# Putting three attention groups together: inside the attention stage, or after it

## The chip, the cores and the metric

The kernel runs on one core of a Trainium2 chip. Its time is the device time of one execution in microseconds (us). The core has five engines that matter here: TensorE (PE, with its weight loads shown as PEld), VectorE (DVE), ScalarE (ACT), GpSimd (POOL) and SyncE (SP), whose queue issues all transfers between HBM and the on-chip memory in this kernel.

## The reference, cut to what matters

One layer of a trunk: a normalised input, one wide projection, a state-space branch and an attention branch, both gated, merged and projected out. Sequence 2048, model width 1024. The attention branch has three groups of four heads (head size 128). The groups differ in how far apart their keys lie:

```
DILATION_PATTERNS = ((128, 1), (512, 4), (2048, 16))

for gi, (window, dilation) in enumerate(DILATION_PATTERNS):
    o, s = dilated_group_attention(q[:, :, gi], k[:, :, gi], v[:, :, gi], window, dilation)
    outs.append(o); lses.append(s)
alpha = softmax(stack(lses), axis=0)
y = sum(alpha[..., None] * outs, axis=0)          # the three groups of a head slot
...
y_a = y * silu(z_a)
```

A head slot j (0 to 3) is head j of all three groups. Its three outputs are summed with weights that come from the three softmax denominators, position by position, and the sum is multiplied by silu of a gate projection z_a.

## The kernel before, in words

Matrix products run in f32r, with each operand split into a high and a low part and three products in place of one. The normalised input stays on chip (`hhi`, `hlo`); weights come from HBM in raw tiles `w_raw` of 128x512, are split by ScalarE (high part, L67) and VectorE (low part, L68) into `w_hi` and `w_lo`, and are then used for products of 128x512 (`proj`, L132 to L143). A pair of weight strips is four raw tiles. The tag `w_raw` has two buffers, and so have `w_hi` and `w_lo` (two pairs). Tag `ev` (two buffers) serves the tiles that come from or go to HBM in the attention stage: V of a chunk (`load_split`, L842) and the output `acc` of a chunk (L928, L979).

The stages in order of the program: input and projections for the state-space branch, state-space scan with gate strips between, its output gate (glu), the attention stage, the z stage, the output stage.

- Attention stage: `for j in range(4): for g in range(3): self.unit(...)`. A unit (j, g) loads its Q and K weights (`pair`, L827) and goes through four chunks of 512 positions: K projection, V load, Q projection, scores (L914, L970), softmax (L887), transposes (L920 to L923, L973), products with V (L940, L978), then a store of the chunk's sums without denominator to HBM (`numd`, L963 or L981). At its end maxima and denominators go to HBM (`statd`, L871 to L885).
- z stage: `weights_of_groups` (L983) reads the statistics of a slot, works out the three weights per position and stores them in HBM (`fd`). `combine` (L1004) reads, for each quarter of 512 positions and each group, the sums (`cn`) and the weights spread over 128 partitions (`cf`), multiplies and adds on GpSimd (L1028 to L1031) and leaves the slot's whole result in an on-chip tile `cy` of 128x2048. In between, gate strips are projected: `tanh` strips, and `silu` strips (L682 to L699), whose banks are multiplied by a quarter of `cy` (L697) before they are stored to `ya`.

The order of instructions on each engine is made by a planner when the program is built: it follows the order of the program where nothing else decides, takes what is ready in its own reckoning of the time, and gives each tile one of the buffers of its tag. On the chip each engine works through its own list in that fixed order, and each instruction waits for those on other engines that it depends on. SP issues transfers in its own fixed order as well, and one that has to wait holds up those behind it.

Of the kernel before, what the change touches and what calls it, by code (L numbers as in the profile page):

```python
# [20 lines left out]
SEQ = 2048  # L21
# [18 lines left out]
class Builder:  # L40
# [641 lines left out]
    def gate_bank(self, ev, psum, w, s, q, dst, silu=False, factor=None):  # L682

        nc = self.nc
        t = {}

        def product():
            t["ps"] = psum.tile([128, 512], F32, tag="proj", name="proj")
            return self.proj(t["ps"], w, s, self.pos(q))

        def evict():
            e = t["e"] = ev.tile([128, 512], F32, tag="ev", name="ze" if silu else "ge")
            nc.scalar.activation(e, t["ps"], AF.Tanh, scale=0.5)  # L693
            if silu:
                nc.vector.scalar_tensor_tensor(e, e, 1.0, t["ps"], op0=ALU.add, op1=ALU.mult)
            if factor is not None:
                nc.vector.tensor_tensor(e, e, factor[:, q * 512 : q * 512 + 512], op=ALU.mult)  # L697

        return product, evict, lambda: nc.sync.dma_start(dst[q], t["e"])  # L699

# [202 lines left out]
    def banded_chunk(self, g, c, carry, qh, ql, kh, kl, vh, vl, prev, st, pool, ev, psum, dst):  # L903
        nc = self.nc
        ph, pl = (pool.tile([128, 8, 128], F32R, name=n) for n in ("ph", "pl"))
        for pair in range(2):
            s = psum.tile([128, 2, 256], F32, tag="s", name="s")
            t = psum.tile([128, 4, 128], F32, tag="t", name="t")
            lone = pair == 0 and not carry
            for h in range(2):  # L910
                b = 2 * pair + h
                k0 = 1 if b == 0 and not carry else b
                for n, (x, y) in enumerate(((qh, kh), (qh, kl), (ql, kh))):
                    nc.tensor.matmul(s[:, h], x[:, b], y[:, k0 : k0 + 2], start=n == 0, stop=n == 2)  # L914
            for h in range(2):
                b = 2 * pair + h
                first = b == 0 and not carry
                p = self.softmax(s[:, h], self.mask[:, 128:384] if first else self.mask[:, 0:256], 4 * c + b, st, pool)
                if first:
                    nc.tensor.transpose(t[:, 1], p[:, 0:128], self.ident)  # L920
                else:
                    nc.tensor.transpose(t[:, 2 * h], p[:, 0:128], self.ident)
                    nc.tensor.transpose(t[:, 2 * h + 1], p[:, 128:256], self.ident)  # L923
            i0 = 1 if lone else 0
            sl = slice(4 * pair + i0, 4 * pair + 4)
            self.split(ph[:, sl], pl[:, sl], t[:, i0:])
# [8 lines left out]
        def blocks(x):  # L935
            return x.rearrange("p b (i r) -> p b i r", r=width)
# [9 lines left out]
        nb = psum.tile([128, 4, 128], F32, tag="n", name="nb")  # L946
        pv(nb[:, 0:2], (vh[:, 1], vl[:, 1]), 3)
        pv(nb[:, 2:4], (vh[:, 2], vl[:, 2]), 5)
        lo = pool.tile([128, 4, 128], F32, name="nlo")
        if carry:  # L950
            nc.scalar.activation(lo[:, 0:2], na[:, 0::3], AF.Copy)
        else:
            nc.scalar.activation(lo[:, 1], na[:, 3], AF.Copy)
        nc.scalar.activation(lo[:, 2:4], nb[:, 1::2], AF.Copy)
        if carry:
            nc.vector.tensor_tensor(dest[:, 0], blocks(na[:, 2:3])[:, 0], blocks(lo[:, 0:1])[:, 0], op=ALU.add)
        else:
            nc.vector.tensor_copy(dest[:, 0], blocks(na[:, 2:3])[:, 0])
        nc.vector.tensor_tensor(dest[:, 1:3], blocks(nb[:, 0::2]), blocks(lo[:, 1:3]), op=ALU.add)
        nd = psum.tile([128, 2, 128], F32, tag="n", name="nd")  # L960
        pv(nd, (vh[:, 3], vl[:, 3]), 6)
        nc.vector.tensor_tensor(dest[:, 3], blocks(nd[:, 1:2])[:, 0], blocks(lo[:, 3:4])[:, 0], op=ALU.add)
        nc.sync.dma_start(dst, acc)  # L963

    def causal_chunk(self, c, q, k, v, st, pool, ev, psum, dst):
# [14 lines left out]
        nc.scalar.activation(acc, n.rearrange("p b i -> p (b i)"), AF.Copy)  # L980
        nc.sync.dma_start(dst, acc)  # L981

    def weights_of_groups(self, j, pool, statd, fd):  # L983

        nc = self.nc
        m = pool.tile([16, 6, 128], F32, name="cm")
        nc.sync.dma_start(m, statd[j].rearrange("g s (r i) -> r (g s) i", r=16))
        mx = pool.tile([16, 128], F32, name="cx")
        nc.vector.tensor_tensor(mx, m[:, 0], m[:, 2], op=ALU.max)
        nc.vector.tensor_tensor(mx, mx, m[:, 4], op=ALU.max)  # L990
        e = pool.tile([16, 3, 128], F32, name="ce")
        for g in range(3):
            nc.vector.tensor_tensor(e[:, g], m[:, 2 * g], mx, op=ALU.subtract)
        nc.scalar.activation(e, e, AF.Exp, scale=HEAD_SCALE)
        t = pool.tile([16, 3, 128], F32, name="ct")
        nc.vector.tensor_tensor(t, e, m[:, 1::2], op=ALU.mult)
        nc.vector.tensor_tensor(mx, t[:, 0], t[:, 1], op=ALU.add)
        nc.vector.tensor_tensor(mx, mx, t[:, 2], op=ALU.add)
        nc.vector.reciprocal(mx, mx)
        for g in range(3):  # L1000
            nc.vector.tensor_tensor(e[:, g], e[:, g], mx, op=ALU.mult)
        nc.sync.dma_start(fd[j].rearrange("g (r i) -> r g i", r=16), e)

    def combine(self, j, pool, numd, fd):  # L1004

        nc = self.nc
        y = pool.tile([128, SEQ], F32, name="cy", bufs=2)
        for q in range(4):
            qs = slice(512 * q, 512 * q + 512)
            yo = y[:, qs]  # L1010
            for g in range(3):
                f = pool.tile([128, 512], F32, name="cf", bufs=2)
                nc.sync.dma_start(f, fd[j, g : g + 1, qs].to_broadcast([128, 512]))
                n = pool.tile([128, 512], F32, name="cn", bufs=3)
                if g == 0:
                    src = numd[j, 0].rearrange("c p (h x) -> h p c x", h=4)[q]
                    nc.sync.dma_start(n.rearrange("p (c x) -> p c x", c=4), src)
                    vn = n.rearrange("p (c r i) -> p r c i", c=4, r=4)
                    vf, vy = (t.rearrange("p (r c i) -> p r c i", r=4, c=4) for t in (f, yo))
                elif g == 1:  # L1020
                    src = numd[j, 1].rearrange("c p (h x) -> h p c x", h=4)[q]
                    nc.sync.dma_start(n.rearrange("p (c x) -> p c x", c=4), src)
                    vn, vf, vy = n, f, yo
                else:
                    nc.sync.dma_start(n, numd[j, 2, q])
                    vn, vf, vy = n, f, yo
                if g == 0:
                    nc.gpsimd.tensor_tensor(vy, vn, vf, op=ALU.mult)  # L1028
                else:
                    nc.gpsimd.tensor_tensor(vn, vn, vf, op=ALU.mult)  # L1030
                    nc.gpsimd.tensor_tensor(vy, vy, vn, op=ALU.add)  # L1031
        return y


    def weight_tiles(self, pool, name, kt, cols=(0, D_MODEL)):
# [97 lines left out]
    def run(self, stop=None):  # L1133
        tc, nc, a = self.tc, self.nc, self.a
        with (
# [11 lines left out]
            numd = dp.tile([4, 3, 4, 128, 512], F32, name="numd")  # L1147
            statd = dp.tile([4, 3, 2, SEQ], F32, name="statd")
            fd = dp.tile([4, 3, SEQ], F32, name="fd")
            self.vd = dp.tile([3, SEQ, 512], F32, name="vd")  # L1150
            self.ident = cst.tile([128, 128], F32, name="ident")
            make_identity(nc, self.ident)
# [8 lines left out]
            with tc.tile_pool(name="w", bufs=2, **T) as wp, tc.tile_pool(name="ev", bufs=2, **T) as ev:  # L1161
# [35 lines left out]
                if stop == "glu":  # L1197
                    return
                with tc.tile_pool(name="at", bufs=1, **T) as ap:
                    self.mask = ap.tile([128, 384], F32, name="mask")  # L1200
                    nc.sync.dma_start(self.mask, a["mask"])
                    for j in range(4):
                        for g in range(3):
                            self.unit(j, g, wp, ap, ev, psum, numd, statd)
                if stop == "att":
                    return

                def emit(banks):
                    for bank in banks:
                        for step in bank:  # L1210
                            step()
# [1 line left out]
                def tanh(c):  # L1213
                    emit(self.tanh_pair(ev, psum, self.pair(wp, IDX_GA + c, IDX_GA + c + 1), gta[c : c + 2]))

                with tc.tile_pool(name="cb", bufs=1, **T) as cp:
                    for j in range(4):
                        self.weights_of_groups(j, cp, statd, fd)
                    for p in range(2):
                        y = [self.combine(j, cp, numd, fd) for j in (2 * p, 2 * p + 1)]  # L1220
                        if p == 0:
                            tanh(0)
                        tanh(2 + 2 * p)
                        i = IDX_ZA + 2 * p
                        emit(self.silu_pair(ev, psum, self.pair(wp, i, i + 1), ya[2 * p : 2 * p + 2], y))
                if stop == "ya":
                    return
                with tc.tile_pool(name="bs", bufs=1, **T) as bp:
# [14 lines left out]
def prepare(x, pre_norm_g, w_in, lambda_re, lambda_im, log_dt, b_re, b_im, c_re, c_im, d_skip, w_glu, b_glu,  # L1243
# [15 lines left out]
    never = np.full((128, 128), NEG)  # L1259
    mask = np.concatenate([before, own, never], 1)  # L1260
    diag0 = np.zeros((16, 8, 16))
    diag0[np.arange(16), 0, np.arange(16)] = 1.0
    return {
# [31 lines left out]
```

## Time and profile before

| | |
|---|---|
| time, median of 3 runs | 2094.47 us (2093.51 to 2095.44) |
| profiled execution | 2099.32 us, span 2097.5 us |
| TensorE busy | 2054.6 us (98%) |
| VectorE, ScalarE, GpSimd busy | 901.2, 592.8, 399.2 us |
| mean granted clock of TensorE | 0.992 |

The attention stage lies at about 750 to 1450 us of the span, the z stage at about 1450 to 1720. A busy TensorE is counted from the start of a product to its modelled end; products overlap, so a full share need not be its peak. The granted clock is 1.00 at 2.4 GHz.

### The profile page before, as it was taken

How to read it: one execution, taken by the hardware profiler on the slowest of the kernel's cores; microseconds unless marked ns; L12 is line 12 of the kernel's file. 1: busy time of each engine (PE TensorE's matmuls, PEld its weight loads, DVE VectorE, ACT ScalarE, POOL GpSimd, SP SyncE). 2: the span in 40 equal slices, each digit the busy share in tenths (PEclk: the TensorE clock that was granted, in tenths of full speed). 3: DMA queues.
4: the chain of work that ended last, by engine and by line, in shares of the span. 5: the costliest groups of instructions: out<-in, count | busy, mean ns of one | idle time of the engine just before them, and what ended most of it. 6: DMA issues, size and time to landing. Idle time of an engine off the chain costs nothing.

```text
span 2097.5 us, 30805 instructions
## 1 busy us (share of the span) xinstructions
PE 2054.6 (98%) x11668; PEld 1789.9 (85%) x11668; DVE 901.2 (43%) x2261; ACT 592.8 (28%) x1327; POOL 399.2 (19%) x384
## 2 busy tenths in 40 slices
PE   8999999999999999999999999999899999999998
PEld 6788888899999988888888888887677888999997
DVE  6882355645442234324424423433311226544434
ACT  6421122222223334334433433432111124112111
POOL 0002355555521210000000000000636101111111
PEclk9999999999999999999999999999999999999999
DMA  7334333343345521111111121113747336433323
GB/s 246 106 122 143 97 119 113 117 117 113 114 119 174 151 71 55 59 56 56 61 56 52 41 65 52 59 54 111 217 145 225 111 122 220 141 121 116 117 81 101
DMA packets 208372, 231.50 MB, mean 110 GB/s; under 512 B 24864, under 2 KB 142944, under 8 KB 207968
## 3 DMA queue, kind: packets, MB, share of 16 engines
q1 hardware_dynamic: 208224, 229.54, 35.5%
q8 instruction: 91, 1.49, 0.3%
q14 instruction: 57, 0.47, 0.1%
HBM read 146.52 MB, written 74.56 MB: 105 GB/s over the span
## 4 chain that ended last, share of the span: by engine, by line
PE 86%; DMA 7%; DVE 2%; ACT 1%; POOL 1%; issue 1%; SPq 1%; DVEq 0%; ACTq 0%; POOLq 0%
PE proj L141 46%; PE pv L163 13%; PE br L1089 8%; PE po L1108 8%; DMA cf<-fd 2%; PE glu L786 2%; PE s L914 2%; PE nb L940 1%; DMA raw<-in_wout_dram 1%; PE na L940 1%; DMA cn<-numd 1%; PE nc L978 1%; POOL cn L1030 1%; PE py L598 1%; PE s L970 1%; PE pd L561 1%
## 5 line engine op out<-in xcount | busy, mean ns | idle before, releaser
L141 PE MATMUL proj<-hhi,w_hi 128*128 128x512 f32 x1664 | 666.6, 402 | 25.6 <-ACT ge L693 15.5
L141 PE MATMUL proj<-hlo,w_hi 128*128 128x512 f32 x1664 | 660.9, 398 | 3.2 <-DVE hlo L68 2.7
L141 PE MATMUL proj<-hhi,w_lo 128*128 128x512 f32 x1664 | 660.1, 397 | 0.0
L141 PEld LDWEIGHTS proj<-hhi,w_hi 128*128 128x128 f32 x1664 | 316.2, 190 | 95.8 <-ACT ge L693 17.8
L141 PEld LDWEIGHTS proj<-hlo,w_hi 128*128 128x128 f32 x1664 | 316.1, 190 | 71.6 <-DVE hlo L68 3.4
L141 PEld LDWEIGHTS proj<-hhi,w_lo 128*128 128x128 f32 x1664 | 315.8, 190 | 65.5
L163 PE MATMUL pv<-w_hi,hhi 128*128 128x256 f32 x768 | 218.8, 285 | 0.0
L163 PE MATMUL pv<-w_hi,hlo 128*128 128x256 f32 x768 | 214.5, 279 | 0.0
L163 PE MATMUL pv<-w_lo,hhi 128*128 128x256 f32 x768 | 214.5, 279 | 0.0
L68 DVE TENSOR_TENSOR w_lo<-w_raw,w_hi 128x512 fp32r<-128x512 f32 (+1 forms) x130 | 108.1, 855 | 209.2 <-ACT w_hi L67 208.6
L163 PEld LDWEIGHTS pv<-w_hi,hhi 128*128 128x128 f32 x768 | 144.4, 188 | 0.6
L163 PEld LDWEIGHTS pv<-w_lo,hhi 128*128 128x128 f32 x768 | 144.4, 188 | 0.6
L163 PEld LDWEIGHTS pv<-w_hi,hlo 128*128 128x128 f32 x768 | 144.3, 188 | 0.0
L898 ACT ACTIVATE p<-p,nm 128x256 f32<-128x256 f32 (+1 forms) x192 | 89.5, 467 | 152.0 <-DVE nm L897 135.9
L892 DVE CUSTOM_DVE_ANT_0 p<-s,mask 128x256 f32<-128x256 f32 (+1 forms) x192 | 68.2, 376 | 147.1 <-PE t L973 68.7
L1092 POOL TENSOR_TENSOR gt<-gt 128x256 f32<-128x256 f32 x64 | 48.3, 759 | 386.1 <-DVE gt L1091 221.3
L67 ACT ACTIVATE w_hi<-w_raw 128x512 fp32r<-128x512 f32 (+1 forms) x130 | 77.1, 620 | 124.6 <-DMA w_raw<-in_wst_dram 87.5
L848 POOL CAST kh<-kh 128x128 fp32r<-128x128 f32 x12 | 3.6, 296 | 538.2 <-PE s L970 426.3
L1108 PE MATMUL po<-wout0h,mh 128*128 128x512 f32 x256 | 98.9, 392 | 1.6 <-ACT wout0h L67 1.4
L1108 PE MATMUL po<-wout0l,mh 128*128 128x512 f32 x256 | 99.8, 390 | 0.0
L1108 PE MATMUL po<-wout0h,ml 128*128 128x512 f32 x256 | 99.5, 390 | 0.0
L693 ACT ACTIVATE ge<-proj 128x512 f32<-128x512 f32 x64 | 37.8, 593 | 192.1 <-PE proj L141 136.9
(248 smaller groups left out, 3341.8 us busy)
## 6 DMA issues: line engine op xcount, KB each, us to landing
w_raw<-in_wst_dram SPq DMA_DIRECT2D x126, 256.0 KB
vd<-ve SPq DMA_DIRECT2D x48, 256.0 KB
numd<-acc SPq DMA_DIRECT2D x48, 256.0 KB
cn<-numd SPq DMA_DIRECT2D x48, 256.0 KB
cf<-fd SPq DMA_DIRECT2D x48, 256.0 KB
xT<-in_xT_dram SPq DMA_DIRECT2D x32, 256.0 KB
gts<-ge SPq DMA_DIRECT2D x32, 256.0 KB
sx<-sx SPq DMA_DIRECT2D x64, 128.0 KB
```

Source lines behind the costliest of these rows:

```text
L67: nc.scalar.activation(hi, src, AF.Copy)
L68: nc.vector.tensor_tensor(lo, src, raw(hi), op=ALU.subtract)
L141: last = nc.tensor.matmul(ps, st[:, k, cs], m, start=n == 0, stop=n == 23)
L163: last = nc.tensor.matmul(ps[:, o], st[:, k, rs], m[:, k], start=n == 0, stop=n == 23)
L786: nc.tensor.matmul(ps, st[:, k, cs], m[:, k], start=n == 0, stop=n == 11)
L892: nc.vector.tensor_tensor_reduce(p[:, :n], scores, mask, scale=1.0, scalar=-3.0e38, op0=ALU.add, op1=ALU.max, accum_out=st[:, 0, blk : blk ...
L898: nc.scalar.activation(p[:, :n], p[:, :n], AF.Exp, scale=HEAD_SCALE, bias=nm, accum_out=st[:, 1, blk : blk + 1])
L914: nc.tensor.matmul(s[:, h], x[:, b], y[:, k0 : k0 + 2], start=n == 0, stop=n == 2)
L940: nc.tensor.matmul(out, x, y[:, i0 : i0 + 2], start=n == 0, stop=n == 2)
L1089: nc.tensor.matmul(ps, st[:, k, cs], m[:, i, k], start=n == 0, stop=n == 11)
L1092: nc.gpsimd.tensor_tensor(gt[:, 0], gt[:, 0], gt[:, 1], op=ALU.add)
L1108: nc.tensor.matmul(po[b, half], st[:, k, bs], m[:, k, hs], start=k == 0 and n == 0, stop=k == 7 and n == 2,)
```

## The change

Combining moves into the attention stage: right behind the three units of slot j, `combine(j)` works out the weights, and for each of eight pieces of 256 positions and each group loads weights and sums into one tile, multiplies and adds on GpSimd, and stores the sum to HBM (`yad`). The tile of a piece takes tag `w_raw`. The z strips load the quarter that they need from `yad` into one of three buffers. The weights are worked out on 128 partitions of 16 positions, not 16 of 128. The first block of a sequence has 128 keys only, so its scores and mask are cut to 128 columns, and the third mask block goes. `nlo` shrinks to two blocks, used twice in a chunk.

```diff
-                nc.vector.tensor_tensor(e, e, factor[:, q * 512 : q * 512 + 512], op=ALU.mult)
+                nc.vector.tensor_tensor(e, e, factor(q), op=ALU.mult)
...
-                k0 = 1 if b == 0 and not carry else b
+                lead = b == 0 and not carry
+                out, ks = (s[:, h, :128], slice(1, 2)) if lead else (s[:, h], slice(b, b + 2))
                 for n, (x, y) in enumerate(((qh, kh), (qh, kl), (ql, kh))):
-                    nc.tensor.matmul(s[:, h], x[:, b], y[:, k0 : k0 + 2], start=n == 0, stop=n == 2)
+                    nc.tensor.matmul(out, x[:, b], y[:, ks], start=n == 0, stop=n == 2)
...
-        nc.scalar.activation(lo[:, 2:4], nb[:, 1::2], AF.Copy)
...
-        nc.vector.tensor_tensor(dest[:, 1:3], blocks(nb[:, 0::2]), blocks(lo[:, 1:3]), op=ALU.add)
+        nc.vector.tensor_tensor(dest[:, 1], blocks(nb[:, 0:1])[:, 0], blocks(lo[:, 1:2])[:, 0], op=ALU.add)
+        lo = pool.tile([128, 2, 128], F32, name="nlo")
+        nc.scalar.activation(lo, nb[:, 1::2], AF.Copy)
+        nc.vector.tensor_tensor(dest[:, 2], blocks(nb[:, 2:3])[:, 0], blocks(lo[:, 0:1])[:, 0], op=ALU.add)
...
+    def combine(self, j, wp, pool, numd, statd, fd, yd):
...
+        m = pool.tile([128, 6, 16], F32, name="cm")
+        nc.sync.dma_start(m, statd[j].rearrange("g s (p x) -> p (g s) x", x=16))
...
+        nc.sync.dma_start(fd[j].rearrange("g (p x) -> p g x", x=16), e)
         for q in range(4):
+            for o in (0, 256):
+                y = pool.tile([128, 256], F32, name="cy")
+                for g in range(3):
+                    r = wp.tile([128, 2, 256], F32, tag="w_raw", name="cnf", bufs=2)
+                    f, n = r[:, 0], r[:, 1]
+                    at = 512 * q + o
+                    nc.sync.dma_start(f, fd[j, g : g + 1, at : at + 256].to_broadcast([128, 256]))
+                    if g == 0:
+                        src = numd[j, 0].rearrange("c p (h x) -> h p c x", h=8)[2 * q + o // 256]
+                        nc.sync.dma_start(n.rearrange("p (c x) -> p c x", c=4), src)
...
+                        nc.gpsimd.tensor_tensor(vy, vn, vf, op=ALU.mult)
+                    else:
...
+                        nc.gpsimd.tensor_tensor(n, n, f, op=ALU.mult)
+                        nc.gpsimd.tensor_tensor(y, y, n, op=ALU.add)
+                nc.sync.dma_start(yd[j, q][:, o : o + 256], y)
...
                     for j in range(4):
                         for g in range(3):
                             self.unit(j, g, wp, ap, ev, psum, numd, statd)
+                        self.combine(j, wp, ap, numd, statd, fd, yad)
...
-                with tc.tile_pool(name="cb", bufs=1, **T) as cp:
-                    for j in range(4):
-                        self.weights_of_groups(j, cp, statd, fd)
+                with tc.tile_pool(name="za", bufs=1, **T) as zp:
+
+                    def mixed(j, q):
+                        f = zp.tile([128, 512], F32, name="cy", bufs=3)
+                        nc.sync.dma_start(f, yad[j, q])
+                        return f
...
-                        y = [self.combine(j, cp, numd, fd) for j in (2 * p, 2 * p + 1)]
```

## Rows read from the trace of the kernel before

**Rows 1.** The page, busy us of each engine, share of the span, instructions.

```profile
PE 2054.6 (98%) x11668; PEld 1789.9 (85%) x11668; DVE 901.2 (43%) x2261; ACT 592.8 (28%) x1327; POOL 399.2 (19%) x384
```

**Rows 2.** Windows of 50 us: stretch, length, busy per engine, clock, DMA share, GB/s.

```profile
850.00:900.00 50.00, 50.00 (x264) 42.25 (x263) 17.47 (x65) 18.95 (x54) 0.00 (x0) 1.00 0.20 64
...
1450.00:1500.00 50.00, 43.28 (x182) 35.10 (x183) 27.91 (x50) 7.39 (x15) 25.07 (x20) 0.97 0.66 190
1500.00:1550.00 50.00, 47.02 (x196) 38.32 (x195) 3.25 (x4) 6.98 (x12) 29.50 (x23) 0.93 0.73 212
1550.00:1600.00 50.00, 46.84 (x200) 38.30 (x199) 15.05 (x20) 6.87 (x12) 22.45 (x17) 0.97 0.53 163
1600.00:1650.00 50.00, 46.67 (x200) 38.26 (x200) 5.84 (x9) 9.33 (x16) 26.94 (x22) 0.97 0.70 209
1650.00:1700.00 50.00, 50.00 (x223) 41.40 (x222) 14.13 (x21) 8.81 (x15) 0.00 (x0) 1.00 0.26 90
```

**Rows 3.** Windows of 5 us in the z stage, the same columns.

```profile
1500.00:1505.00 5.00, 2.51 (x12) 1.73 (x10) 0.02 (x1) 0.68 (x2) 4.04 (x4) 0.95 0.89 215
1505.00:1510.00 5.00, 4.51 (x11) 3.55 (x12) 1.93 (x2) 1.55 (x3) 2.96 (x3) 0.50 1.02 348
```

**Rows 4.** Chain of waits, 1500 to 1520 us: start, us, what.

```profile
1511.92 4.34 DMA cf<-fd
```

**Rows 5.** Timeline of SP's queue, 780 to 860 us: start, us, instruction, count.

```profile
782.46 0.32 SPq L963 DMA_DIRECT2D numd<-acc  x1
784.44 0.37 SPq L100 DMA_DIRECT2D ev<-vd  x1
...
801.35 0.94 SPq L100 DMA_DIRECT2D w_raw<-in_wst_dram  x2
...
806.17 1.19 SPq L100 DMA_DIRECT2D w_raw<-in_wst_dram  x2
...
859.48 0.93 SPq L100 DMA_DIRECT2D w_raw<-in_wst_dram  x2
```

**Rows 6.** Timelines of VectorE and ScalarE, 778 to 863 us; in brackets idle before, and releaser.

```profile
778.20 0.69 DVE L68 TENSOR_TENSOR vl<-ev,vh 128x512 fp32r<-128x512 f32 x1 [0.80 <-ACT vh L67]
...
790.65 0.38 DVE L956 TENSOR_TENSOR acc<-na,nlo 128x128 f32<-128x128 f32 x1
...
858.09 1.15 ACT L67 ACTIVATE w_hi<-w_raw 128x512 fp32r<-128x512 f32 x2 [1.01 <-PE proj L141]
...
862.16 0.63 ACT L67 ACTIVATE w_hi<-w_raw 128x512 fp32r<-128x512 f32 x1 [0.17 <-DMA w_raw<-in_wst_dram]
```

**Rows 7.** Timeline, 1434 to 1458 us: the end of the last attention unit.

```profile
1434.57 0.58 ACT L862 ACTIVATE q<-proj 128x512 f32<-128x512 f32 x1
...
1439.24 1.05 PE L970 MATMUL s<-k,q 128*128 128x128 f32 x8
...
1441.00 0.40 ACT L898 ACTIVATE p<-p,nm 128x128 f32<-128x128 f32 x1 [1.99 <-DVE nm L897]
...
1448.43 0.34 SPq L885 DMA_DIRECT2D statd<-stt  x1
1448.87 0.37 SPq L987 DMA_DIRECT2D cm<-statd  x1
...
1456.21 0.32 SPq L1002 DMA_DIRECT2D fd<-ce  x1
...
1457.78 0.85 SPq L1013 DMA_DIRECT2D cf<-fd  x2
```

**Rows 8.** Instructions that touch `cx`: ns min/median/max, first and last start.

```profile
L989 DVE TENSOR_TENSOR cx<-cm x4: 278/280/1292, 1450.8 to 1477.5; 16x128 f32<-16x128 f32 x4
```

**Rows 9.** Groups of GpSimd instructions: shape, count, busy us, mean ns, idle before.

```profile
L793 POOL TENSOR_TENSOR glu_z<-glu_z,glu_t 128x256 f32<-128x256 f32 x32 | 24.2, 755 | 107.8 <-DVE glu_t L792 93.2 <-DMA vd<-ve 11.7 <-DMA glu_z<-zs 2.3
```

**Rows 10.** Timeline of TensorE at 760 us.

```profile
760.07 0.28 PE L914 MATMUL s<-kh,qh 128*128 128x256 f32 x1
760.19 0.28 PE L914 MATMUL s<-kl,qh 128*128 128x256 f32 x1
```

More of the change, by code (lines that the diff above doesn't have):

```diff
@@ L917, in banded_chunk @@
                 first = b == 0 and not carry
-                p = self.softmax(s[:, h], self.mask[:, 128:384] if first else self.mask[:, 0:256], 4 * c + b, st, pool)
+                if first:
+                    p = self.softmax(s[:, h, :128], self.mask[:, 128:256], 4 * c + b, st, pool)
+                else:
+                    p = self.softmax(s[:, h], self.mask, 4 * c + b, st, pool)
                 if first:
@@ L948, in banded_chunk @@
         pv(nb[:, 2:4], (vh[:, 2], vl[:, 2]), 5)
-        lo = pool.tile([128, 4, 128], F32, name="nlo")
+        lo = pool.tile([128, 2, 128], F32, name="nlo")
         if carry:
-            nc.scalar.activation(lo[:, 0:2], na[:, 0::3], AF.Copy)
+            nc.scalar.activation(lo, na[:, 0::3], AF.Copy)
+            nc.vector.tensor_tensor(dest[:, 0], blocks(na[:, 2:3])[:, 0], blocks(lo[:, 0:1])[:, 0], op=ALU.add)
         else:
             nc.scalar.activation(lo[:, 1], na[:, 3], AF.Copy)
-        nc.scalar.activation(lo[:, 2:4], nb[:, 1::2], AF.Copy)
-        if carry:
-            nc.vector.tensor_tensor(dest[:, 0], blocks(na[:, 2:3])[:, 0], blocks(lo[:, 0:1])[:, 0], op=ALU.add)
-        else:
             nc.vector.tensor_copy(dest[:, 0], blocks(na[:, 2:3])[:, 0])
-        nc.vector.tensor_tensor(dest[:, 1:3], blocks(nb[:, 0::2]), blocks(lo[:, 1:3]), op=ALU.add)
+        nc.vector.tensor_tensor(dest[:, 1], blocks(nb[:, 0:1])[:, 0], blocks(lo[:, 1:2])[:, 0], op=ALU.add)
+        lo = pool.tile([128, 2, 128], F32, name="nlo")
+        nc.scalar.activation(lo, nb[:, 1::2], AF.Copy)
+        nc.vector.tensor_tensor(dest[:, 2], blocks(nb[:, 2:3])[:, 0], blocks(lo[:, 0:1])[:, 0], op=ALU.add)
         nd = psum.tile([128, 2, 128], F32, tag="n", name="nd")
         pv(nd, (vh[:, 3], vl[:, 3]), 6)
-        nc.vector.tensor_tensor(dest[:, 3], blocks(nd[:, 1:2])[:, 0], blocks(lo[:, 3:4])[:, 0], op=ALU.add)
+        nc.vector.tensor_tensor(dest[:, 3], blocks(nd[:, 1:2])[:, 0], blocks(lo[:, 1:2])[:, 0], op=ALU.add)
         nc.sync.dma_start(dst, acc)
@@ L981, in causal_chunk @@
         nc.sync.dma_start(dst, acc)
-    def weights_of_groups(self, j, pool, statd, fd):
+    def combine(self, j, wp, pool, numd, statd, fd, yd):
         nc = self.nc
-        m = pool.tile([16, 6, 128], F32, name="cm")
-        nc.sync.dma_start(m, statd[j].rearrange("g s (r i) -> r (g s) i", r=16))
-        mx = pool.tile([16, 128], F32, name="cx")
+        m = pool.tile([128, 6, 16], F32, name="cm")
+        nc.sync.dma_start(m, statd[j].rearrange("g s (p x) -> p (g s) x", x=16))
+        mx = pool.tile([128, 16], F32, name="cx")
         nc.vector.tensor_tensor(mx, m[:, 0], m[:, 2], op=ALU.max)
         nc.vector.tensor_tensor(mx, mx, m[:, 4], op=ALU.max)
-        e = pool.tile([16, 3, 128], F32, name="ce")
+        e = pool.tile([128, 3, 16], F32, name="ce")
         for g in range(3):
@@ L994, in weights_of_groups @@
         nc.scalar.activation(e, e, AF.Exp, scale=HEAD_SCALE)
-        t = pool.tile([16, 3, 128], F32, name="ct")
+        t = pool.tile([128, 3, 16], F32, name="ct")
         nc.vector.tensor_tensor(t, e, m[:, 1::2], op=ALU.mult)
@@ L1001, in weights_of_groups @@
             nc.vector.tensor_tensor(e[:, g], e[:, g], mx, op=ALU.mult)
[L1002 to L1007, printed above, removed]
+        nc.sync.dma_start(fd[j].rearrange("g (p x) -> p g x", x=16), e)
         for q in range(4):
[L1009 to L1032, printed above, removed]
@@ new lines, in combine @@
+            for o in (0, 256):
[8 more added lines that the diff above has]
+                        nc.sync.dma_start(n.rearrange("p (c x) -> p c x", c=4), src)
+                        vn = n.rearrange("p (c r i) -> p r c i", c=4, r=2)
+                        vf, vy = (x.rearrange("p (r c i) -> p r c i", r=2, c=4) for x in (f, y))
+                        nc.gpsimd.tensor_tensor(vy, vn, vf, op=ALU.mult)
+                    else:
+                        if g == 1:
+                            src = numd[j, 1].rearrange("c p (h x) -> h p c x", h=4)[q][:, o // 128 : o // 128 + 2]
+                            nc.sync.dma_start(n.rearrange("p (c x) -> p c x", c=2), src)
+                        else:
+                            nc.sync.dma_start(n, numd[j, 2, q][:, o : o + 256])
+                        nc.gpsimd.tensor_tensor(n, n, f, op=ALU.mult)
+                        nc.gpsimd.tensor_tensor(y, y, n, op=ALU.add)
+                nc.sync.dma_start(yd[j, q][:, o : o + 256], y)
@@ L1149, in run @@
             fd = dp.tile([4, 3, SEQ], F32, name="fd")
+            yad = dp.tile([4, 4, 128, 512], F32, name="yad")
             self.vd = dp.tile([3, SEQ, 512], F32, name="vd")
@@ L1199, in run @@
                 with tc.tile_pool(name="at", bufs=1, **T) as ap:
-                    self.mask = ap.tile([128, 384], F32, name="mask")
+                    self.mask = ap.tile([128, 256], F32, name="mask")
                     nc.sync.dma_start(self.mask, a["mask"])
@@ L1224, in run @@
                         i = IDX_ZA + 2 * p
-                        emit(self.silu_pair(ev, psum, self.pair(wp, i, i + 1), ya[2 * p : 2 * p + 2], y))
+                        factor = [lambda q, j=j: mixed(j, q) for j in (2 * p, 2 * p + 1)]
+                        emit(self.silu_pair(ev, psum, self.pair(wp, i, i + 1), ya[2 * p : 2 * p + 2], factor))
                 if stop == "ya":
@@ L1258, in prepare @@
     own, before = np.where(to <= at, 0.0, NEG), np.where(to >= at, 0.0, NEG)
-    never = np.full((128, 128), NEG)
-    mask = np.concatenate([before, own, never], 1)
+    mask = np.concatenate([before, own], 1)
     diag0 = np.zeros((16, 8, 16))
```

## The prediction

> **What bounds the kernel now.** I read the page's busy shares first: TensorE has work for 98% of the span and the next engine, VectorE, for 43% [rows 1]. So time is won only where TensorE waits or runs at its lower clock, and lost wherever it is made to wait. The windows say where that is: whole stretches of the attention stage show 50.00 of 50 us busy at granted clock 1.00, while the four windows from 1450 to 1650 us, in which the three groups are put together, show 43.28, 47.02, 46.84 and 46.67 us and clocks of 0.97, 0.93, 0.97, 0.97 [rows 2]. In the worst 5 us of it the clock is 0.50, the lower of its two levels (1.2 of 2.4 GHz), right behind 5 us in which TensorE was busy for 2.51 [rows 3]. The chain of waits there runs through the loads `cf<-fd`, 4.34 us each, and the GpSimd products behind them [rows 4]. After 1650 us the z strips run without a combine beside them at 50.00 and 1.00 [rows 2].
>
> So the stage that the change empties loses 6.72 + 2.98 + 3.16 + 3.33 = 16.2 us of idle time and at most 50 x (0.03 + 0.07 + 0.03 + 0.03) = 8 us of clock; some of the low clock falls on idle time, so I take 6. **What there is to gain is 22 us** (bounds 14 and 24).
>
> **Where the moved work starts, and behind what.** The 24 pieces of a head slot (8 times 256 positions, 3 groups) are held in tiles of tag `w_raw`, of which there are two buffers, and through the same two pass all raw weights. In the program combine(j) stands between the weights of unit (j,2) and those of unit (j+1,0). What decides everything is whether the two buffers are given out in program order, or to whoever can use them first. Tag `ev` answers it. It too has two buffers, and its tiles in program order are V of chunk c, `acc` of c, V of c+1, and so on. V of chunk 1 is done with its buffer at 778.20 + 0.69 = 778.9 us. The load of V for chunk 2 needs nothing but a buffer, and SP is idle; yet it is issued at 784.44, 1.98 us behind the store of `acc` 0 at 782.46, whose buffer it takes. The buffer free since 778.9 is held for `acc` of chunk 1, which is not written before 790.65 [rows 5, 6]. The same 1.98 to 2.06 us between store and load stand behind 11 of the 31 later V loads of the stage. So a buffer goes to the next tile in program order even if that tile cannot be filled for 12 us.
>
> Now the same for `w_raw`. Today the weights of the next unit but one are fetched long before use: two raw tiles at 806.17, split at 858.09 when the unit running lets go of `w_hi`, the other two loaded at 859.48 and split from 862.16 [rows 5, 6]. With the change the two buffers that fall free at about 806 belong to the first two pieces of combine(j), which can't be filled before the statistics of unit (j,2) are stored, some 130 us later. Behind them stand 22 more pieces, and behind those the weights of unit (j+1,0). When unit (j,2) ends, TensorE has no product left that it could make: every later one needs those weights. After j = 3 the same holds for the first tanh strips. **Four stalls**, each worked out here from the last Q product of unit (j,2):
>
> - End of the unit. In the trace it takes from 1434.57 (copy of q) to 1448.43 (store of the statistics), but with foreign projections in between [rows 7]. Its own steps are the copy 0.58, the scores 1.05, four exponentials of 0.40 with their sums read out [rows 7], the links between them, transposes and copies: by estimate 6.5 us, in which TensorE works about 3.5. Idle: 3.
> - Statistics out and in: a store must land before its reader is issued, 1.98 as for `acc` [rows 5], and the load reaches VectorE 1.93 later (1448.87 to the first `cx` at 1450.8 [rows 7, 8]). The factors take 1450.8 to 1456.2 today, 5.4 us on 128 elements per partition [rows 7, 8]; now 12 VectorE instructions have 16 or 48. Between 12 x 0.15 and 5.4, I take 3. Storing `fd` and issuing the next load: 1456.21 to 1457.78, 1.57 [rows 7]. Landing of the first piece 2.7, as for 256 KB of weights, 859.48 to 862.16 [rows 5, 6]. Sum 11.2.
> - The pieces. A GpSimd product on 256 elements takes 0.76 us [rows 9]. Refilling a buffer (semaphore, two issues, landing) I put at 3.1, the 2.7 of one weight load and a second issue of 0.4 [rows 5, 6]. With the first group's product at 0: it ends at 0.76, product and sum of the second at 2.3; the third group's tile refills the first buffer from 0.76, is there at 3.9 and done at 5.4; then `y`, which has one buffer, must be stored and land (2.0) before the next piece may start at 7.5. Eight pieces less the last landing: 8 x 7.5 - 2 = 58. From below, GpSimd's five operations and two buffers at 3.1 allow about 42; from above, the combine of today at its worst, 3.5 us a group in a full DMA system, and 2 for `y`, gives 100.
> - Weights: four raw tiles through the same two buffers, 2.7 to land and 0.63 + 0.69 to split [rows 5, 6]. TensorE starts on the K strip, the third tile, 5.4 after the last sum (after j = 3 on the first strip, 1.4).
> - The clock comes back at its lower level, as at 1505 us, where 4.51 us of work at 0.50 took the place of 2.3 at full clock [rows 3]: 2.5.
>
> 3 + 11.2 + 58 + 5.4 + 2.5 = 80 for j = 0 to 2, and 76 for j = 3: **316 us** (bounds 4 x 60 and 4 x 122). SP issues 58 transfers per slot in this time, some 0.4 each; nothing else is queued there that could go on. The GpSimd copies of kh and kl queue behind the sums, but belong to units that wait as well.
>
> The Trainium skill ("DMA: Bandwidth & Descriptors", Specifications and Why small descriptors are slow) wants at least 512 bytes per piece of a transfer and reckons three cycles beside the 32-byte beats of each; group 0 is now read in pieces of 256. As an estimate from that page, 11 cycles for 256 bytes against 19 for 512 would be up to 0.4 us for each of 32 loads and a sum 13 us higher. No row here shows such a load alone.
>
> **The rest.** The 60 score products of first blocks get 128 columns for 256. Two products of 256 follow each other at 0.12 us (760.07 to 760.19 [rows 10]); the scores of unit (j,2), 128 columns in plain f32, take 1.05 for 8 instructions, 0.13 each and two for a product [rows 7]. So 60 x (0.06 to 0.26 - 0.12) = -4 to +8 us; I take 0, as the instruction at 128 columns costs what that at 256 does. `acc` is written in more, smaller steps through a smaller `nlo`: 32 more VectorE instructions of 0.4, beside projections; 0, and 8 if the second `nlo` holds back TensorE by 0.25 in each chunk. The smaller masks shorten VectorE work that nobody waits for. The 16 loads of sums in the z strips are 256 KB each, one per 5.4 us bank, with three buffers: 0, and 2.7 once if that cover is gone.
>
> **Sum.** The profiled execution has span 2097.5 and time 2099.3. 2099.3 + 316 - 22 = 2393; the median of the runs lies 4.9 below that execution, so **2388 us**, 14% slower.
>
> **Rivals.**
> 1. The buffers go to whoever is ready. The weights then go first, combine(j) runs beside the next units, where GpSimd is idle, and only the gain is left: 2099.3 - 22 - 4.9 = 2072, with up to 8 more for SP's queue. For it: DMA and GpSimd are nearly empty in the attention stage [rows 2]. Against it: [rows 5, 6]. It decides at one place, whether `w_raw` loads come before the last statistics of a slot. 10%. Of this case the skill ("SBUF — State Buffer", Who interferes with whom) says that a VectorE instruction with two SBUF inputs and a GpSimd one block each other for a whole instruction; the trace agrees, `cx` takes 0.28 and beside the combine up to 1.29 [rows 8]. VectorE is free half the time there, so it would cost that case little.
> 2. Order of the program, but the pieces go at today's pace, about 100 us a slot: 4 x 42 more, 2557. For it: loads of 4.34 us [rows 4]. Against it: those run beside weights, stores and z strips, at 163 to 212 GB/s [rows 2]; alone, 256 KB land in 2.7. 8%.
> 3. The next unit's weights get through, but the pieces, older in the program, then hold the buffers against the weights of unit (j+1,2): three stalls of about 10 us, 2072 + 30 = 2102, a little slower. 4%.
>
> The forecast has 75%; 3% I can't name. Its own range is 2290 to 2490. With most of rival 2 the range is **2290 to 2540**, which leaves rivals 1 and 3 out. A median of this kernel can be told from no change at about 0.2%. Slower: the forecast and rivals 2 and 3, 0.87; faster: rival 1 and a little of the unnamed, 0.10; same: 0.03.
>
> **What would show it.** Right: four gaps of TensorE, of 65 to 100 us, each behind the last statistics of a slot; in each 24 pieces on GpSimd, and the weights `w_raw` of the next unit issued only after the last piece; busy shares down to about 85%; windows of the z strips at 50.00 and 1.00. Wrong: weights of unit (j+1,0) loaded before the statistics of (j,2), and products of the next slot beside the GpSimd sums. A gap much shorter than 60 us breaks the buffer reckoning, not the order.

## The result, and the profile after

The changed kernel takes **2414.42 us** (median of 4 runs, 2412.11 to 2417.60), the kernel before 2094.95 beside it: ratio 1.1525 (95% interval 1.1511 to 1.1539), 319.5 us slower. The forecast was 2388, with 2290 to 2540 around it. The profiled execution has a span of 2415.8 us at a mean clock of 0.926; [rows 1] had 98% for TensorE, and its line of the page is now:

```profile
PE 2065.4 (85%) x11668; PEld 1794.8 (74%) x11668; DVE 883.7 (37%) x2293; ACT 593.7 (25%) x1327; POOL 411.4 (17%) x464
```

The work is the same, 11,668 products, and TensorE waits. What for, from the waits of TensorE (us in total, times, longest):

```profile
PE proj L141 <- ACT w_hi L67: 314.6, 5, 80.1
...
PE t L978 <- ACT p L898: 5.0, 8, 0.8
PE proj L141 <- ACT ge L693: 3.2, 2, 2.1
PE nc L983 <- DVE pt L980: 2.7, 4, 0.7
...
PE s L975 <- ACT q L862: 1.9, 4, 0.5
```

The first row is the four stalls, 314.3 us, and one small wait. The stalls stand in TensorE's timeline (start, duration, instruction, idle before it and releaser), one behind each slot:

```profile
999.33 0.80 PE L141 MATMUL proj<-hhi,w_hi 128*128 128x512 f32 x1 [79.67 <-ACT w_hi L67]
...
1259.44 0.80 PE L141 MATMUL proj<-hhi,w_hi 128*128 128x512 f32 x1 [79.81 <-ACT w_hi L67]
...
1520.17 0.80 PE L141 MATMUL proj<-hhi,w_hi 128*128 128x512 f32 x1 [80.07 <-ACT w_hi L67]
...
1775.76 0.80 PE L141 MATMUL proj<-hhi,w_hi 128*128 128x512 f32 x1 [74.74 <-ACT w_hi L67]
```

The windows of 50 us [rows 2] show the stalls and, at the end, the z strips, now whole:

```profile
900.00:950.00 50.00, 17.14 (x91) 13.72 (x89) 7.63 (x41) 7.16 (x23) 8.05 (x12) 0.67 0.29 75
950.00:1000.00 50.00, 0.67 (x2) 0.57 (x3) 2.07 (x3) 1.89 (x3) 20.86 (x29) 0.50 0.45 117
...
1800.00:1850.00 50.00, 50.00 (x223) 41.39 (x222) 2.68 (x4) 7.59 (x13) 0.00 (x0) 1.00 0.20 69
```

In a stall GpSimd is the busiest engine with 20.86 of 50 us, and the DMA system is at 0.45: nothing is at its limit, each step waits for the one before. SP's queue in the first stall shows the order (statistics out and in, weights of the groups, pieces, and only then raw weights):

```profile
917.74 0.33 SPq L885 DMA_DIRECT2D statd<-stt  x1
...
920.10 0.37 SPq L993 DMA_DIRECT2D cm<-statd  x1
...
925.40 0.36 SPq L1008 DMA_DIRECT2D fd<-ce  x1
927.07 0.81 SPq L1016 DMA_DIRECT2D cnf<-fd  x2
...
986.04 0.32 SPq L1031 DMA_DIRECT2D yad<-cy  x1
...
991.95 0.34 SPq L100 DMA_DIRECT2D w_raw<-in_wst_dram  x1
993.71 0.32 SPq L1031 DMA_DIRECT2D yad<-cy  x1
994.07 4.52 SPq L100 DMA_DIRECT2D w_raw<-in_wst_dram  x3
```

The first weight is asked for at 991.95, 74.2 us behind the statistics, when the last piece has its tiles and GpSimd lets go of a buffer. It is so in all four stalls: SP waits for GpSimd's sum before the first weight (`SPq L100 <- POOL cy L1030: 6.3, 4, 1.6`, once a slot).

The whole difference: the span is 318.3 us longer. Of this 314.3 lie in these four waits, and 9.6 in the small waits for `p`, `pt` and `q` above (TensorE has nothing to fill the last unit of a slot with); 16.4 less idle time elsewhere (mostly the z strips) goes off, and 10.8 more busy time comes on. Summed over windows of 1 us (busy time times the clock that is missing), the lower clock at the four stalls costs 13.1 us, and 7.5 us of it in the old z stage are gone; the rest of the 10.8 is not traced. Behind the first stall:

```profile
995.00:1000.00 5.00, 0.67 (x2) 0.57 (x3) 2.07 (x3) 1.53 (x3) 0.00 (x0) 0.50 0.49 141
1000.00:1005.00 5.00, 5.00 (x18) 3.94 (x17) 1.39 (x3) 1.49 (x3) 0.00 (x0) 0.72 0.44 125
1005.00:1010.00 5.00, 5.00 (x23) 3.99 (x22) 1.77 (x3) 1.67 (x3) 0.00 (x0) 1.00 0.51 153
```

### The profile page after: what moved, and what is told of

It is laid out like the page before. It is cut to its first block, busy times and chain, and to the rows that moved or that the text cites. A ratio compares the mean times of both kernels' runs of the same rounds, so it can differ in the third digit from the quotient of the medians.

```text
span 2415.8 us, 31177 instructions
## 1 busy us (share of the span) xinstructions
PE 2065.4 (85%) x11668; PEld 1794.8 (74%) x11668; DVE 883.7 (37%) x2293; ACT 593.7 (25%) x1327; POOL 411.4 (17%) x464
## 4 chain that ended last, share of the span: by engine, by line
PE 79%; DMA 13%; POOL 3%; DVE 2%; ACT 2%; issue 1%; SPq 1%; POOLq 0%; DVEq 0%; ACTq 0%
PE proj L141 45%; PE pv L163 11%; PE br L1088 7%; PE po L1107 6%; DMA cnf<-numd 4%; PE glu L786 2%; PE s L915 2%; DMA yad<-cy 2%; DMA w_raw<-in_wst_dram 2%; POOL cnf L1029 1%; DMA cnf<-fd 1%; POOL cy L1030 1%; PE nb L944 1%; DMA raw<-in_wout_dram 1%; POOL cy L1022 1%
## 5 line engine op out<-in xcount | busy, mean ns | idle before, releaser
L67 ACT ACTIVATE w_hi<-w_raw 128x512 fp32r<-128x512 f32 (+1 forms) x130 | 78.0, 621 | 409.2 <-DMA w_raw<-in_wst_dram 377.7
L1022 POOL TENSOR_TENSOR cy<-cnf 128x256 f32<-128x256 f32 x32 | 23.1, 722 | 678.4 <-DMA cnf<-fd 616.7
L898 ACT ACTIVATE p<-p,nm 128x128 f32<-128x128 f32 (+1 forms) x192 | 87.5, 457 | 182.9 <-DVE nm L897 178.6
L892 DVE CUSTOM_DVE_ANT_0 p<-s,mask 128x128 f32<-128x128 f32 (+1 forms) x192 | 65.4, 362 | 136.1 <-PE t L978 37.8
L693 ACT ACTIVATE ge<-proj 128x512 f32<-128x512 f32 x64 | 38.0, 595 | 208.8 <-PE proj L141 191.9
```

The source lines that it names most:

```text
L67: nc.scalar.activation(hi, src, AF.Copy)
L892: nc.vector.tensor_tensor_reduce(p[:, :n], scores, mask, scale=1.0, scalar=-3.0e38, op0=ALU.add, op1=ALU.max, accum_out=st[:, 0, blk : blk ...
L898: nc.scalar.activation(p[:, :n], p[:, :n], AF.Exp, scale=HEAD_SCALE, bias=nm, accum_out=st[:, 1, blk : blk + 1])
```

## Experiments

**Is it the order in `w_raw`?** In e1_late and e2_next the same combine is asked for later, so that the weights of one more unit, or of two, stand ahead of its pieces.

```diff
 for g in range(3):
     self.unit(j, g, wp, ap, ev, psum, numd, statd)
-self.combine(j, wp, ap, numd, statd, fd, yad)
+    if g == 1 and j > 0:                            # e2_next: g == 0
+        self.combine(j - 1, wp, ap, numd, statd, fd, yad)
+tanh(0)
+tanh(2)                                             # e2_next: behind combine(3)
+self.combine(3, wp, ap, numd, statd, fd, yad)
```

> The changed kernel with one line moved: combine(j) stands behind unit (j+1,1) in the program, so its 24 pieces come behind the weights of units (j+1,0) and (j+1,1) for the two w_raw buffers and before those of unit (j+1,2); combine(3) stands behind the first two tanh pairs. Nothing else differs. Program-order theory: the pieces get the buffers some 16 us after the last statistics and are done some 80 us later, before the weights of unit (j+1,2) are due at 116; the four gaps of 75 to 80 us go, and the time is the old one less the idle and clock of the old z stage, 2072 to 2085 us. Rival (the combine inside the attention stage costs by itself, its 58 transfers per slot on SP's queue and its GpSimd sums beside the units): gaps stay wherever it stands, above 2300 us.

> As e1_late, but combine(j) stands behind unit (j+1,0), combine(3) behind the first tanh pair: the pieces come before the weights of unit (j+1,1). Program-order theory: no gap at the end of a slot, but one in front of each unit (j+1,1): pieces and weights are done some 84 us after the last product of the slot, the unit in between covers 58, so 23 to 28 us three times, and about 37 in front of the second tanh pair, where only 43 are covered; with the clock 2150 to 2220 us, 2187 in the middle. Rival (place alone): the same as e1_late.

Measured: e1_late 2136.66 us, ratio to before 1.0208 (1.0194 to 1.0222); e2_next 2243.09, 1.0723 (1.0707 to 1.0739). The long waits are gone in e1_late, 278 us come back, and so the order theory holds: the same pieces, the same tag, another place in the program. In e2_next TensorE waits for weights 22 to 24 us three times and 42.1 once, where 23 to 28 and about 37 were expected. But both came out slower than expected, e1_late 52 us above its range and e2_next 23. e1_late's waits of TensorE are of another kind: in the attention stage its softmax (`p`) comes late, for which the kernel before has no wait, and in the z stage its gates (`ge`), 16.7 us where the kernel before has 15.5:

```profile
PE proj L141 <- ACT ge L693: 16.7, 5, 10.2
PE t L926 <- ACT p L898: 14.1, 5, 5.4
PE t L924 <- ACT p L898: 11.0, 3, 3.7
```

Followed upstream, ScalarE's own waits from 940 to 1010 us begin with `ACT vh L67 <- DMA ev<-vd`, 33.3 us in 4 (0.3 in 1 before): the softmax steps stand behind the split of V on ScalarE, and V is late. SP's queue of e1_late says why:

```profile
955.84 0.45 SPq L968 DMA_DIRECT2D numd<-acc  x1
956.97 0.32 SPq L1031 DMA_DIRECT2D yad<-cy  x1
...
962.48 0.32 SPq L1016 DMA_DIRECT2D cnf<-fd  x1
...
963.98 0.32 SPq L1016 DMA_DIRECT2D cnf<-fd  x1
964.34 0.43 SPq L1019 DMA_DIRECT2D cnf<-numd  x1
964.82 0.50 SPq L100 DMA_DIRECT2D ev<-vd  x1
```

V is issued 9.0 us behind the store whose buffer it takes, 1.98 before [rows 5]; in between stand loads that wait for buffers GpSimd has not let go of.

**How long is the stall, and what paces a piece?** e5_one_piece sums one piece of eight, e4_two_y gives `y` a second buffer.

```diff
-                y = pool.tile([128, 256], F32, name="cy")
+                y = ev.tile([128, 256], F32, tag="ev", name="cy")       # e4_two_y
...
-        for q in range(4):
-            for o in (0, 256):
+        for q in range(1):                                              # e5_one_piece
+            for o in (0,):
...
-                nc.sync.dma_start(yd[j, q][:, o : o + 256], y)
+                for k in range(8):
+                    nc.sync.dma_start(yd[j, k // 2][:, k % 2 * 256 : k % 2 * 256 + 256], y)
```

> The changed kernel with one of eight pieces of a slot summed, and its sum stored in all eight places (the other seven sums are left out). The gaps then hold everything but seven pieces of 8.1 us: 2414 - 4 x 7 x 8.1 = 2187, up to 12 more for the eight stores. If the gap were the wait for statistics or weights and not the pieces, over 2300.

> The changed kernel with y taken from tag ev, two buffers in place of one. If the landing of y's store (2.0 us) is a step of each piece, as the prediction has it, a slot gets 7 x 2.0 us shorter: 2414 - 4 x 14 = about 2358. If loads or SP's issuing set the pace: 2400 to 2414.

Measured: e5_one_piece 2195.04 us, 1.0467 (1.0453 to 1.0481): (2414.4 - 2195.0) / 28 = 7.8 us for each piece left out, and its first wait is 25.97 us in place of 79.67. The pieces make most of the length of the stall; what stays is the way to the first piece and from the last one to the weights. e4_two_y 2415.16, 1.1514 (1.1498 to 1.1530): no gain, where 56 us were expected if the store of `y` were a step of each piece. GpSimd's timeline in the changed kernel, the first products of two pieces, and below it e4_two_y from one piece to the next:

```profile
947.36 0.72 POOL L1022 TENSOR_TENSOR cy<-cnf 128x256 f32<-128x256 f32 x1 [2.29 <-DMA yad<-cy]
...
955.53 0.72 POOL L1022 TENSOR_TENSOR cy<-cnf 128x256 f32<-128x256 f32 x1 [2.52 <-DMA yad<-cy]
```

```profile
946.94 0.72 POOL L1022 TENSOR_TENSOR cy<-cnf 128x256 f32<-128x256 f32 x1 [2.13 <-DMA cnf<-numd]
949.67 0.72 POOL L1029 TENSOR_TENSOR cnf<-cnf 128x256 f32<-128x256 f32 x1 [2.01 <-DMA cnf<-numd]
950.47 0.72 POOL L1030 TENSOR_TENSOR cy<-cy,cnf 128x256 f32<-128x256 f32 x1
951.61 0.72 POOL L1029 TENSOR_TENSOR cnf<-cnf 128x256 f32<-128x256 f32 x1 [0.42 <-DMA cnf<-numd]
952.41 0.72 POOL L1030 TENSOR_TENSOR cy<-cy,cnf 128x256 f32<-128x256 f32 x1
954.94 0.72 POOL L1022 TENSOR_TENSOR cy<-cnf 128x256 f32<-128x256 f32 x1 [1.81 <-DMA cnf<-numd]
957.63 0.72 POOL L1029 TENSOR_TENSOR cnf<-cnf 128x256 f32<-128x256 f32 x1 [1.97 <-DMA cnf<-numd]
```

The wait for `yad` becomes one for `cnf` of nearly the same size. From the end of a tile's last use to the first use of the next tile in its buffer it takes 4.0 us (947.66 to 951.61), 3.8 (951.19 to 954.94) and 4.5 (953.13 to 957.63): three refills a piece through two buffers are as slow by themselves. The bracket names what came last by a little, not what could be taken away.

**The small edits, and the gain in the z stage.** e6_small has only the edits to the first block's columns, the masks and `nlo`; e7_no_combine leaves the whole combine out of the kernel before (the z strips are multiplied by a tile of ones).

```diff
-                    for j in range(4):
-                        self.weights_of_groups(j, cp, statd, fd)
+                    one = cp.tile([128, SEQ], F32, name="one")          # e7_no_combine
+                    nc.gpsimd.memset(one, 1.0)
...
-                        y = [self.combine(j, cp, numd, fd) for j in (2 * p, 2 * p + 1)]
+                        y = [one, one]
```

> The kernel before with the small edits alone: first-block scores and softmax on 128 columns, two mask blocks, nlo of two blocks used twice. Combine and its place are those of before. Forecast by the prediction: 0, between -4 and +16 us, so 2091 to 2111; within 0.2% of before is the likeliest. Rival (the small nlo holds back TensorE in each of 32 chunks): +8 us or more.

> The kernel before with the combine of the three groups left out: no statistics read, no cf and cn loads, no GpSimd sums; the z strips are multiplied by a tile of ones. It prices what there is to gain in the z stage. Prediction: 22 us (14 to 24), so 2073 us, 2071 to 2081. Rival (the z stage waits for its own weights and stores as much as for the combine): less than 10 us gained, above 2085 us.

Measured: e6_small 2094.14, 1.0009 (1.0000 to 1.0017); e7_no_combine 2070.63, 0.9894 (0.9881 to 0.9908), 22.4 us below the runs beside it. For the small edits that is 1.2 us, at most 3.6 by the interval, where 0 was reckoned; for the z stage it is the 22 reckoned.

**Is it SP's order?** e8_pool_queue is e1_late with combine's transfers on GpSimd's own queue; e9_spread leaves them on SP and puts one piece into each chunk.

```diff
-        nc.sync.dma_start(...)          # the seven of combine
+        nc.gpsimd.dma_start(...)        # e8_pool_queue
...
                 self.load_split(ev, "ev", vh, vl, vsrc)
+                piece(4 * g + c)        # e9_spread: one of eight, from the fourth chunk of a slot on
```

> e1_late with one edit: all transfers of combine (statistics, weights, sums, results) are issued from GpSimd's queue, not SP's. Theory: e1_late's remaining 64 us above 2072 come from SP's fixed order: the loads of V, which ScalarE must split before the softmax steps queued behind it, stand on SP behind piece loads and stores that wait for GpSimd (V was issued 8.4 to 13.2 us behind the store before it, 2.0 in the kernel before). With SP free of them: 2070 to 2090. Rival A: the cost is contention of GpSimd's sums with VectorE or of the transfers among each other: stays at 2125 to 2145. Rival B: issuing transfers costs GpSimd so much (58 per slot) that the pieces outlast the one unit that they have beside the next weights: over 2145.

> All transfers on SP as in e1_late, but the pieces are spread: the weights of combine(j-1) are worked out in the second chunk of unit (j,0), and then one piece stands in each of the next eight chunks, right behind the load of V; combine(3) behind tanh(0) and tanh(2) as in e1_late. By SP's order: a piece is through in about 8 us, and the next entry of the unit on SP, the store of acc, is due some 12 us later, so V is held up no more: 2070 to 2095 (the stop in the z stage, about 10 us, may stay). By contention of GpSimd with VectorE, the same sums run beside the same work: 2120 to 2145.

Measured: e8_pool_queue 2137.38, 1.0191 (1.0177 to 1.0205); e9_spread 2155.68, 1.0277 (1.0263 to 1.0291). Both were expected below 2095 and by the times fall on the rivals' side, e9_spread above even their ranges; only the traces separate the reasons. In e8_pool_queue TensorE's waits for `p` are down from 25.1 to 2.2 us, and those for weights are back, 15.6 us of them in the attention stage and 23.0 in the z stage (first row of its waits):

```profile
PE proj L141 <- ACT w_hi L67: 38.8, 5, 23.0
```

GpSimd issues a transfer in 0.54 to 0.84 us of its own time (medians by kind) and a piece takes longer, as from 959.42 to 970.50 (11.1 us on average, 8.1 in the changed kernel):

```profile
959.42 0.74 POOL L1022 TENSOR_TENSOR cy<-cnf 128x256 f32<-128x256 f32 x1 [1.20 <-DMA yad<-cy]
960.46 0.58 POOL L1016 DMA_DIRECT2D cnf<-fd  x1 [0.30 <-POOL cy L1022]
961.03 0.54 POOL L1028 DMA_DIRECT2D cnf<-numd  x1
...
970.50 0.74 POOL L1022 TENSOR_TENSOR cy<-cnf 128x256 f32<-128x256 f32 x1 [0.97 <-DMA yad<-cy]
```

The eight pieces, from 947.97 to 1033.56, outlast the time until the weights behind them are due: rival B, at a lower price than it was given. No transfer of combine is on SP here, and still the next weights go out only at 1036.23, behind the last sum. That speaks for the buffers as the cause, and against pieces that stand before the weights in SP's list. e9_spread settles nothing: the planner moved the piece loads ahead of V again, and V stands 8.0 us behind the store (956.88 to 964.84), as in e1_late.

**Both orders mended.** e10_halves cuts each combine in two, with the weights of a unit between; e11_halves_sp is the same on SP.

```diff
 if j and g == 1:
-    self.combine(j - 1, wp, ap, numd, statd, fd, yad)
+    self.combine(j - 1, ap, statd, fd)                                  # the weights of the groups
+    self.pieces(j - 1, wp, ap, numd, fd, yad, (0, 1))
+if j and g == 2:
+    self.pieces(j - 1, wp, ap, numd, fd, yad, (2, 3))
...
+self.combine(3, ap, statd, fd)                                          # behind tanh(0), tanh(2)
+self.pieces(3, wp, ap, numd, fd, yad, (0, 1))
+za = self.pair(wp, IDX_ZA, IDX_ZA + 1)
+t4 = self.pair(wp, IDX_GA + 4, IDX_GA + 5)                              # e12_z_order, e13_raw_queue
+self.pieces(3, wp, ap, numd, fd, yad, (2, 3))
```

> e8_pool_queue with each combine cut in two: the weights of the groups and four pieces behind unit (j+1,1), as there, the other four pieces behind unit (j+1,2); combine(3): four pieces before the weights of the first z strips, four behind them. In e8_pool_queue a piece takes 10.8 us on GpSimd's queue (86 a slot), and the next weights, behind the eighth, come 10 to 24 us late, four times. Four pieces are 43 us. Theory (order on SP for V, order in w_raw for weights, nothing else): no stop is left, 2070 to 2090, below the kernel before. If four halves still come late, or GpSimd beside VectorE costs TensorE time: 2100 to 2135.

> e10_halves with all transfers of combine on SP again. By the theory the halves cure only the wait for weights, which e1_late hardly had, and V still queues on SP behind pieces: 2115 to 2145. If it comes below 2095, SP's order is not the cause of e1_late's loss.

Measured: e10_halves 2094.46, 0.9992 (0.9981 to 1.0002), the time of the kernel before and 4 us above what was expected; e11_halves_sp 2131.40, 1.0161 (1.0147 to 1.0175), as expected. Between these two the queue alone differs, and it is worth 37 us. In e11_halves_sp a V goes out 9.2 us behind the store before it (957.01 to 966.25), in e10_halves the same one 2.0 (953.19 to 955.20). In e10_halves the attention stage is whole while GpSimd sums and issues beside it:

```profile
950.00:1000.00 50.00, 50.00 (x274) 42.57 (x273) 24.88 (x79) 21.65 (x55) 31.30 (x50) 1.00 0.54 127
1000.00:1050.00 50.00, 50.00 (x274) 42.66 (x273) 20.47 (x65) 19.11 (x50) 29.07 (x44) 1.00 0.50 127
...
1550.00:1600.00 50.00, 35.28 (x145) 28.96 (x146) 14.75 (x22) 8.98 (x15) 2.03 (x3) 0.80 0.51 160
```

So neither GpSimd beside VectorE nor the transfers beside each other cost TensorE anything there. What is lost is one stop of 17.4 us in the z stage, last row. e12_z_order and e13_raw_queue go after it; e13_raw_queue is e12_z_order and:

```diff
-            self.nc.sync.dma_start(r, src[sl])          # load_split
+            self.raw_queue.dma_start(r, src[sl])        # GpSimd's from combine(3) to tanh(6), else SP's
```

> e10_halves with one edit: the weights of the third tanh pair are asked for before the last four pieces of combine(3), not behind them. In e10_halves the attention stage is whole (50.00 of 50 us at 1.00 in ten windows running), and one stop of 17.4 us is left at about 1550 us: the raw weights of that pair wait in w_raw for the last pieces, and on SP the loads of y for the first z strips stand behind them. Theory: with them ahead the stop goes, and the 15 us of lower clock behind it: 2094 - 17 - 3 = 2074, range 2070 to 2085, faster than the kernel before. Rival: the pieces, now later, hold up something else (the y of slot 3, the next weights): 2088 or more.

> e12_z_order with one edit: in the z stage the raw weights of the first z strips, the third tanh pair and the second z strips are issued from GpSimd's queue too, in the program's order with the pieces that share their two buffers. In e12_z_order the third load of the second z strips' weights stood on SP from 1531 to 1574 us, waiting for a buffer that the pieces held, and behind it the loads of y and the stores of the z strips, which waited for nothing else (TensorE stopped for 32.4 us). Theory: on GpSimd's queue it holds up nothing, the stop goes: 2110 - 32 - 4 of clock = 2074, range 2068 to 2085, faster than the kernel before. Rival: the stop was the pieces' own lateness and comes back at another place: 2090 or more.

Measured: e12_z_order 2110.52, 1.0075 (1.0061 to 1.0088), a miss: the stop grew to 32.4 us. Its SP queue shows the same thing once more, raw weights held up for 43 us with the loads of y behind them:

```profile
1530.89 43.42 SPq L100 DMA_DIRECT2D w_raw<-in_wst_dram  x3
1574.41 1.37 SPq L1235 DMA_DIRECT2D cy<-yad  x3
```

e13_raw_queue, where whatever waits for these two buffers stands in one queue: **2089.44, 0.9964 (0.9951 to 0.9977)**, 0.36% below the kernel before, the one version with all its work whose interval lies below 1. It was expected at 2068 to 2085. The stop is 11.3 us now, and its cause has moved to the lists of ScalarE and VectorE. There the two steps that evict a z bank (L693 on ScalarE, L695 on VectorE) stand behind the split of weights, which the last pieces still hold up:

```profile
1580.61 0.63 ACT L67 ACTIVATE w_hi<-w_raw 128x512 fp32r<-128x512 f32 x1 [17.59 <-DMA w_raw<-in_wst_dram]
...
1583.08 0.58 ACT L693 ACTIVATE ze<-proj 128x512 f32<-128x512 f32 x1
...
1581.27 0.69 DVE L68 TENSOR_TENSOR w_lo<-w_raw,w_hi 128x512 fp32r<-128x512 f32 x1 [16.80 <-ACT w_hi L67]
...
1583.81 0.68 DVE L695 SCALAR_TENSOR_TENSOR ze<-ze,proj 128x512 f32<-128x512 f32 x1
```

Buffers of their own for the pieces, which would test the cause most directly and should take it away, were not tried: the stage's on-chip memory has no room for two.

## Why the prediction was right, point by point

The mechanism was the one forecast: four stalls, one behind each slot, because the pieces, older in the program, hold the buffers of the next weights. e1_late shows that the order is the cause (same work, 278 us less), e5_one_piece that the pieces make up most of its length. Rival 1 and rival 3 are refuted for this kernel by the timeline of SP, rival 2 by the pace.

The sizes, per stall, for j = 0:

| step | forecast, us | measured |
|---|---|---|
| end of the unit, idle | 3 | 0.5: waits of 9.6 / 4 = 2.4, less 1.9 (917.74 to 919.66) in which TensorE still works behind the statistics |
| statistics to first product | 11.2 | 13.2 (917.74 to 930.97) |
| pieces | 58 | 62.7 (930.97 to 993.71) |
| weights | 5.4 | 5.6 (993.71 to 999.33) |
| clock | 2.5 | 2.7 (busy time times the missing clock; 3.3 on the mean of the four) |

- In the way to the first product, the factors took 2.9 (forecast 3, 922.49 to 925.40); the first tile took 3.9 to arrive, not 2.7, and the store and load of the statistics 2.4 each, not 1.98 and 1.93.
- **The term most off is the pieces**: 8.1 us each (`yad` from 937.09 to 993.71, seven steps), not 7.5, and by another step than I had. "y, which has one buffer, must be stored and land before the next piece may start" is not what paces them; e4_two_y took that away and nothing changed. The refills do, at 3.8 to 4.5 us each where I had 3.1. So it is in part luck that the term came so near: with refills of 3.1 and no wait for `y` the prediction's own lower figure for a slot was about 42.
- By the medians a stall costs (319.5 + 22.4) / 4 = 85.5 us, forecast 79 on average. The waits are (314.3 + 9.6) / 4 = 81.0 of it. Of the 4.5 that remain, 13.1 / 4 = 3.3 are the lower clock, of the restart (0.50 and 0.72 in the two windows shown) and of the last products of a slot; 1.2 are not traced.
- The gain in the z stage, 22, and the small edits, 0, were confirmed apart, 22.4 and none. 4 x (85.5 - 79) = 26 is the whole miss.
- The extra for short pieces that the Trainium skill gives ("DMA: Bandwidth & Descriptors", Why small descriptors are slow), 13 us in all by an estimate, would close half of it. The trace of e4_two_y does not show it. There, from the issue of a load of sums to the product that waits for it, group 0 (pieces of 256 bytes) takes 3.50 us on the median of 28, group 2 (1,024 bytes) 3.53 on that of 29, and group 1 (512 bytes) 3.91 on that of 32: the shortest pieces are not the slowest.
- **What was wrong is rival 1's price.** "2072, with up to 8 more for SP's queue": with the weights ahead it took 2137. SP's fixed order then holds V back, and the queue alone is worth 37 us (e11_halves_sp to e10_halves). I had SP's 58 transfers a slot at 0.4 us each and did not ask who stands behind one that waits for GpSimd.
- A small slip: the 1.98 to 2.06 us between store and load stand behind 12 later V loads, not 11; the reading of `ev` does not change by it.

## What to carry to other kernels

When new work is given buffers of a tag that the critical loads use, ask first what stands between in program order: a buffer is promised to the next tile, however late that can be filled. The same question holds for a queue: a transfer that waits stops all behind it, so transfers that wait for one slow engine belong in one queue with whatever else waits for it, and away from those that wait for nothing. And a releaser in brackets is the last of several; take it away before you believe it.

## What the runs showed of the hardware

Issued from GpSimd, a transfer of combine costs 0.54 to 0.84 us of GpSimd's time (e8_pool_queue, medians by kind), against 0.32 to 0.44 of SP's for the same ones (e1_late), and a piece takes 11.1 us in place of 8.1. Beside GpSimd's sums, VectorE's split of V, with both inputs in SBUF (the on-chip memory of the tiles), took 1017 ns on the mean of 7 (e13_raw_queue, 940 to 1045 us) in place of 692 on the mean of 8 in the kernel before. That agrees with the Trainium skill ("SBUF — State Buffer", Who interferes with whom), by which a VectorE instruction with two SBUF inputs and a GpSimd instruction that reads SBUF block each other for a whole instruction. In the same run the four windows of 50 us from 900 to 1100 us show TensorE at 50.00 and 1.00, so it cost TensorE nothing there.
